# Constant matrix products, cued by results, in the recurrence of a two-layer decoder trunk

## The chip, the cores and the metric

The kernel runs on one core of a Trainium2 chip. Its time is the device time of one execution in microseconds (us). The kernel before was timed three times: 3217.7, 3225.27 and 3227.76 us, median 3225.27 us. The core has a matrix engine (PE; its weight loads are listed as PEld), a vector engine (DVE), an engine for activations and copies (ACT), a general one (POOL), and SP, whose queue issues nearly all DMA transfers. Each engine works through its instructions in order and waits at semaphores.

## The reference

Two layers over 1024 positions of width 1024. Each layer has a token mixer, a cross-attention into 256 memory rows and a SwiGLU network, each wrapped in RMS norms. Layer 0 mixes with a gated MLP, layer 1 with the recurrence that matters here:

```python
def rwkv7_recurrence(r, w, k, v, a, b):
    """S_t = S_{t-1} diag(w_t) + (S_{t-1} a_t) b_t^T + v_t k_t^T ;  y_t = S_t r_t."""
    def step(S, inp):
        r_t, w_t, k_t, v_t, a_t, b_t = inp
        sa = jnp.einsum('bhij,bhj->bhi', S, a_t)
        S = S * w_t[:, :, None, :] + sa[..., None] * b_t[:, :, None, :] + v_t[..., None] * k_t[:, :, None, :]
        return S, jnp.einsum('bhij,bhj->bhi', S, r_t)
    ...
y = rwkv7_recurrence(rh, decay, kh, vh, -kk, kk * ah)
mu = jnp.mean(y, axis=-1, keepdims=True)
var = jnp.mean(jnp.square(y - mu), axis=-1, keepdims=True)
y = (y - mu) * lax.rsqrt(var + RW_GN_EPS)
...
y = y + jnp.sum(rh * kh * r_k, axis=-1, keepdims=True) * vh
return (y * g) @ w_o
```

There are 16 heads of 64 values. The kernel computes the recurrence in chunks of 64 positions instead of step by step.

## The kernel before, in words

The large projections run as streams of 128x512 products, three for each pair of tiles (`mm3`, lines 148 to 150: high part by high part and the two mixed ones, in fp32r), and set most of the time. The recurrence works in four batches `b` of 256 positions, each with four groups `pi` of four heads. A batch goes through these steps, each written as a generator:

- `rwkv_prep`: loads the five inputs, forms the decay by a scan (L1295) and two exponentials (L1298, L1299), copies the decay of each chunk's end to `D` (L1302), builds the scaled tiles `ar` and `bk` (L1307 to L1311), and on PE a head sum (L1318), the chunk's inner products (L1330), transposes (L1337) and a product into `uv` (L1354). All PE products here are small and in fp32.
- `rwkv_solve`: inverts 32x32 triangles on DVE, 31 steps, two at a time for all heads, and stores the inverses.
- `rwkv_merge`: loads the inverses (`x<-scr` on L1393, `z<-scr` on L1398) and joins them to 64x64 with two rounds of 32x32 products (L1410, L1419), with copies between by ACT (L1413, L1422).
- `rwkv_chunks`: the sequential part over four chunks of eight states (L1433, L1446), with evacuations on ACT (L1453, L1462, L1465) and DVE (L1447).
- `rwkv_post`: the norm of the output. Sums (L1498, L1499), difference (L1502), squares (L1507), sums (L1511), a power on POOL (L208), products on POOL (L1503, L1513), transposes on PE (L1520, L1527), scaling on ACT and DVE (L1524, L1528, L1529), and a store (L1530).

After the chunks of batch `b - 1` and the solve of batch `b`, the loop runs the preparation of batch `b + 1` with the norm of batch `b - 1` in the background, and then the merge of batch `b`. So the span has three kinds of stretch: chunks; after the first and the second chunks a turn with norm, preparation and merge together; and, for the last batch, a merge between output projections.

Tiles in PSUM come from two rotating sets of four banks during the recurrence, `ps` (`bank`) and `ck` (`bank_ck`). A scheduler in the compiler places the instructions of each engine in an order that it estimates itself, so one more instruction can move its neighbours. SP's queue is in order too: a load that waits for a buffer holds those behind it.

## Time and profile before

| | us |
|---|---|
| median of three runs | 3225.27 |
| profiled execution, time | 3225.86 |
| profiled execution, span from first to last instruction | 3224.2 |
| PE busy in the span | 3085.9 |
| DVE busy | 1825.7 |
| ACT busy | 1485.6 |
| POOL busy | 824.9 |
| mean granted PE clock (1 is full) | 0.966 |

A row of a timeline has its start, its length, the engine, the source line, the operation, the tiles written and read, and the count of what was merged into the row; in brackets stands the engine's idle time before it and what ended it. In the rows by stretch each engine has its busy time and its count of instructions; the number after the five engines is the clock that PE was granted. A matrix product in fp32 is recorded as two.

### The profile page before, as it was taken

Reading aid. Unit: us, or ns where it says so; the run is one execution under the profiler, and the core shown is the slowest. Engines: PE = TensorE matmul, PEld = TensorE weight load, DVE = VectorE, ACT = ScalarE, POOL = GpSimd, SP = SyncE. Lnnn points to the kernel's source line nnn. Section 1 sums busy time; section 2 is a strip of 40 time slices with the busy share of each in tenths; the row PEclk is TensorE's granted clock in tenths of the full one; section 3 lists DMA queues with packets and bytes.
Section 4 is the critical chain, followed back from the end, with each engine's and each line's share of the span. In section 5 each row is a group of like instructions: output and inputs, shape, how many; then the busy total and the mean of one; then the engine's idle time right before and its main releaser. Section 6 shows DMA issues by size and latency. Waiting matters only on the chain.

```text
span 3224.2 us, 43854 instructions
## 1 busy us (share of the span) xinstructions
PE 3085.9 (96%) x16570; PEld 2523.5 (78%) x16570; DVE 1825.7 (57%) x2562; ACT 1485.6 (46%) x2751; POOL 824.9 (26%) x646
## 2 busy tenths in 40 slices
PE   8999999899999999999989999999999899999998
PEld 6888888778888777878767778787788678888776
DVE  5563544565555476655765665664545755554656
ACT  5442544543333345666653445455545533333443
POOL 0100011355555100111421121223011555554001
PEclk9999999999999999999998888899999999999999
DMA  5622634423333644744857642535544333333633
GB/s 188 207 77 67 201 122 161 144 66 104 105 98 99 243 142 131 222 122 151 260 190 194 192 107 81 153 96 179 175 153 142 100 102 98 98 98 114 237 112 134
DMA packets 432499, 456.54 MB, mean 142 GB/s; under 512 B 77664, under 2 KB 307200, under 8 KB 432288
## 3 DMA queue, kind: packets, MB, share of 16 engines
q1 hardware_dynamic: 425376, 428.57, 42.2%
q0 software_dynamic: 6912, 25.17, 2.4%
q8 instruction: 131, 2.15, 0.3%
q14 instruction: 80, 0.66, 0.1%
HBM read 331.43 MB, written 122.22 MB: 141 GB/s over the span
## 4 chain that ended last, share of the span: by engine, by line
PE 83%; DVE 7%; DMA 4%; ACT 2%; issue 2%; POOL 1%; SPq 1%; DVEq 0%; POOLq 0%; ACTq 0%
PE ps L438 25%; PE ps L148 12%; PE ps L149 12%; PE ps L150 12%; PE ps L639 11%; PE ck L1433 4%; DVE wl L119 2%; PE ps L1330 2%; PE ck L1446 1%; PE ps L1354 1%; DVE a L119 1%; ACT wh L118 1%; PE ps L262 1%; DMA a<-scr 1%; PE ps L1337 1%
## 5 line engine op out<-in xcount | busy, mean ns | idle before, releaser
L438 PE MATMUL ps<-a,wh 128*128 128x512 f32 x2464 | 772.6, 399 | 7.2 <-DVE a L119 5.0
L119 DVE TENSOR_TENSOR wl<-wr,wh 128x1024 fp32r<-128x1024 f32 (+1 forms) x417 | 478.9, 1158 | 485.9 <-ACT wh L118 477.7
L118 ACT CAST wh<-wr 128x1024 fp32r<-128x1024 f32 (+1 forms) x417 | 371.3, 902 | 621.7 <-PE ps L639 172.6
L438 PEld LDWEIGHTS ps<-a,wh 128*128 128x128 f32 x2464 | 465.6, 189 | 125.6 <-DVE a L119 7.3
L438 PE MATMUL ps<-a,wl 128*128 128x512 f32 x1232 | 480.3, 398 | 0.0
L148 PE MATMUL ps<-a,wh 128*128 128x512 f32 (+1 forms) x848 | 329.1, 393 | 11.3 <-ACT a L118 8.0
L149 PE MATMUL ps<-a,wh 128*128 128x512 f32 (+1 forms) x848 | 326.2, 386 | 2.4 <-DVE a L119 2.4
L148 PE MATMUL ps<-wh,a 128*128 128x512 f32 x800 | 316.4, 403 | 12.3 <-DVE a L1528 3.9
L150 PE MATMUL ps<-a,wl 128*128 128x512 f32 (+1 forms) x848 | 325.0, 385 | 0.8 <-DVE wl L119 0.8
L149 PE MATMUL ps<-wl,a 128*128 128x512 f32 x800 | 319.2, 399 | 0.8 <-DVE wl L119 0.8
L150 PE MATMUL ps<-wh,a 128*128 128x512 f32 x800 | 317.2, 400 | 0.0
L208 POOL TENSOR_TENSOR sm<-sm,mhalf 128x4 f32<-128x4 f32 (+3 forms) x60 | 70.0, 1170 | 922.0 <-DVE sm L228 846.4
L438 PEld LDWEIGHTS ps<-a,wl 128*128 128x128 f32 x1232 | 233.2, 189 | 57.3 <-DVE wl L119 0.9
L639 PE MATMUL ps<-wl,wh 128*128 128x512 f32 x588 | 233.0, 396 | 11.6 <-DVE wl L119 11.6
L119 DVE TENSOR_TENSOR wl<-s,wh 128x512 fp32r<-128x512 f32 x176 | 201.1, 1156 | 68.4 <-ACT wh L118 64.7
L639 PE MATMUL ps<-wh,wl 128*128 128x512 f32 x588 | 230.9, 393 | 0.0
L639 PE MATMUL ps<-wh 128*128 128x512 f32 x588 | 195.3, 395 | 15.1 <-ACT wh L118 15.1
L118 ACT CAST wh<-s 128x512 fp32r<-128x512 f32 x176 | 106.3, 620 | 201.8 <-PE ps L438 66.9
L148 PEld LDWEIGHTS ps<-a,wh 128*128 128x128 f32 x848 | 163.0, 193 | 44.0 <-ACT a L118 9.0
L148 PEld LDWEIGHTS ps<-wh,a 128*128 128x128 f32 x800 | 152.3, 191 | 49.5 <-DVE a L1528 4.3
L150 PEld LDWEIGHTS ps<-a,wl 128*128 128x128 f32 x848 | 163.0, 192 | 35.4 <-DVE wl L119 2.3
L149 PEld LDWEIGHTS ps<-a,wh 128*128 128x128 f32 x848 | 163.4, 193 | 32.9 <-DVE a L119 2.7
(280 smaller groups left out, 5338.2 us busy)
## 6 DMA issues: line engine op xcount, KB each, us to landing
scr<-a SPq DMA_DIRECT2D x218, 256.0 KB
wr<-in_ffn_w_in SPq DMA_DIRECT2D x90, 512.0 KB
wr<-scr SPq DMA_DIRECT2D x70, 512.0 KB
scr<-t SPq DMA_DIRECT2D x60, 512.0 KB
wr<-in_rw_w_rkv SPq DMA_DIRECT2D x48, 512.0 KB
a<-in_ffn_w_out SPq DMA_DIRECT2D x40, 512.0 KB
t<-scr SPq DMA_DIRECT2D x36, 512.0 KB
ld<-scr SPq DMA_DIRECT2D x72, 256.0 KB
```

What stands on the lines that cost most here:

```text
L118: self.nc.scalar.copy(hi, src)
L119: (engine or self.nc.vector).tensor_sub(lo, src, hi)
L148: nc.tensor.matmul(out, lhsT=ah, rhs=bh, start=start, stop=False)
L149: nc.tensor.matmul(out, lhsT=ah, rhs=bl, start=False, stop=False)
L150: nc.tensor.matmul(out, lhsT=al, rhs=bh, start=False, stop=stop)
L208: self.nc.gpsimd.tensor_tensor(out=r, in0=v, in1=self.mhalf[:, 0:n], op=ALU.pow)
L262: nc.tensor.transpose(ps[:, t * P:(t + 1) * P], xs[t][:, k * P:(k + 1) * P], self.ident)
L438: self.nc.tensor.matmul(out, lhsT=a, rhs=b, start=start and k == 0 and (i == 0), stop=k == 3 and i == 2, skip_group_check=True)
L639: nc.tensor.matmul(ps, lhsT=a, rhs=b, start=i in (1, 2, 5) and n == 0 and k == 0 and z == 0, stop=n == NS - 1 and k == steps[n][1] - 1 and ...
L1330: nc.tensor.matmul(ps[:, c * P:(c + 1) * P], lhsT=BK[hs, q * 4 + c, :, :], rhs=AR[hs, q * 4 + c, :, :], start=True, stop=True)
L1337: nc.tensor.transpose(ps[:, c * P:(c + 1) * P], BK[:, q * 4 + c, :, :], self.ident)
L1433: mm = lambda o, l, r: nc.tensor.matmul(o, lhsT=l, rhs=r, start=False, stop=True, skip_group_check=True)
```

## The change

A tile `fill` of 128x128 ones in bf16 is set at the start. A new function `dense(n, cue)` copies one column of `cue` into the first column of `fill` on ACT and then issues `n` products of `fill` with itself, read four times over (512 columns), into a fresh `ps` bank. Nothing reads that bank. The copy makes the products wait until `cue` is there; the value itself is used nowhere.

It is called in three places: in the preparation of batches 2 and 3 when `D` is there (six products), in every merge after the first of the four copies between its two rounds (six), and in the norm of batches 0 and 1 when the means are there (four). That is 8 × 6 + 4 × 6 + 8 × 4 = 104 products.

```diff
+        self.fill = self.const.tile([P, P], BF16, name='fill')
+        nc.gpsimd.memset(self.fill, 1.0)
...
+    def dense(self, n, cue):
+
+        nc = self.nc
+        nc.scalar.copy(self.fill[0:cue.shape[0], 0:1], cue)
+        ps = self.bank()
+        for _ in range(n):
+            nc.tensor.matmul(ps, lhsT=self.fill, rhs=self.fill.rearrange('p (o c) -> p o c', o=1).broadcast_to([P, 4, P]), start=True, stop=True)
...
@@ rwkv_prep
-        T = B['T'][pi] = {}
+        T, b_ = ({}, b)
+        B['T'][pi] = T
...
         nc.vector.tensor_copy(T['D'], ck(ee)[:, :, 63])
+        if b_ > 1:
+            self.dense(6, T['D'][:, 0:1])
...
@@ rwkv_merge
         for pi in range(4):
             nc.scalar.copy(tt[pi // 2][hi[pi], :], pb[pi][hi[pi], :])
             yield
+            if pi == 0:
+                self.dense(6, tt[0][hi[0], 0:1])
...
@@ rwkv_post
         nc.vector.tensor_scalar_mul(mu, mu, 1.0 / 64)
+        if b < 2:
+            self.dense(4, mu[:, 0:1])
```

The new lines shift the numbers: L1318 becomes L1331, L1330 L1343, L1337 L1350, L1354 L1367, L1393 L1406, L1398 L1411, L1410 L1423, L1520 L1537, L1527 L1544; the new products are on L113. Ahead of the recurrence the order of all engines is the same but for the memset. Three places show what moves.

PE at the end of the first chunks, where the turn begins. Before, from the first head sum of batch 2's preparation on (`sel` is its constant, `a` are norm tiles, `x` the inverses for the merge):

```order
L1318 MATMUL ps<-sel,ld 128x2 x4
L1330 MATMUL ps<-ar,bk 128x128 x8
L1520 MATMUL ps<-ident,a 128x128 x4
L1527 MATMUL ps<-ident,a 128x128 x4
L1337 MATMUL ps<-ident,bk 128x128 x4
L1520 MATMUL ps<-ident,a 128x128 x4
L1410 MATMUL ck<-x_15494 32x32 x12
```

Now, from the last product of the fourth norm's burst on:

```order
L113 MATMUL ps<-fill 128x512
L1343 MATMUL ps<-ar,bk 128x128 x4
L1537 MATMUL ps<-ident,a 128x128 x4
L1544 MATMUL ps<-ident,a 128x128 x4
L1350 MATMUL ps<-ident,bk 128x128 x4
L1537 MATMUL ps<-ident,a 128x128 x4
L1544 MATMUL ps<-ident,a 128x128 x4
L1343 MATMUL ps<-ar,bk 128x128 x4
L1537 MATMUL ps<-ident,a 128x128 x4
L1544 MATMUL ps<-ident,a 128x128 x4
L1343 MATMUL ps<-ar,bk 128x128 x4
L1423 MATMUL ck<-x_15560 32x32 x40
```

The merge's first products now stand behind two more groups of L1343 and behind the transposes of three norms instead of one and a half. Ahead of the head sum (now L1331) stand two norm bursts among the last chunk products and, directly before it, six and four products more, 18 in all; the fourth norm's four follow it after four products of L1343.

SP at the same turn, around the second load of the merge. Before (`invX` is the solve's result, `uv` a load for the preparation):

```order
L1384 DMA scr_9774<-invX 16x16x32 x4
L1495 DMA a<-scr_9792 128x2x128 x2
L1292 DMA ld<-scr_9787 128x2x256
L1393 DMA x_15494<-scr_9774 128x512
L1398 DMA z_14040<-scr_9773 32x16x32 x4
```

Now:

```order
L1397 DMA scr_9776<-invX 16x16x32 x4
L1510 DMA a<-scr_9794 128x2x128 x2
L1303 DMA ld<-scr_9789 128x2x256
L1361 DMA uv<-scr_9794 64x4x128 x2
L1303 DMA ld<-scr_9791 128x2x256
L1406 DMA x_15560<-scr_9776 128x512
```

The load of `x` has gone behind two loads of `uv` and one of `ld`. In the second turn its place is unchanged.

PE in the back of the second turn, between two groups of a preparation. Before:

```order
L1337 MATMUL ps<-ident,bk 128x128 x4
L1354 MATMUL ps<-uv,bk 64x64 x16
L1419 MATMUL ck<-z_14040,x1t 32x32 x3
L1318 MATMUL ps<-sel,ld 128x2 x4
L1419 MATMUL ck<-z_14041,x1t 32x32
```

Now:

```order
L113 MATMUL ps<-fill 128x512
L1434 MATMUL ck<-z_14042,x1t 32x32 x9
L1367 MATMUL ps<-uv,bk 64x64 x8
L1331 MATMUL ps<-sel,ld 128x2 x4
L1343 MATMUL ps<-ar,bk 128x128 x4
```

The next preparation's burst of six splits the sixteen products into `uv` in two groups of eight, and some of the merge's second round comes between. The bursts of the other preparations in a turn stand in the same way, and the merge's burst follows the last of them.

## The prediction

> **What bounds the kernel now.** I read the page first, for the share of each engine and the chain that ended last, then the busy time of the engines in stretches of the recurrence, then the PE's own timeline there.
>
> ```profile
> span 3224.2 us, 43854 instructions
> PE   8999999899999999999989999999999899999998
> PEclk9999999999999999999998888899999999999999
> PE 83%; DVE 7%; DMA 4%; ACT 2%; issue 2%; POOL 1%; SPq 1%; DVEq 0%; POOLq 0%; ACTq 0%
> ```
>
> The chain is 83% PE, and one fortieth of the span after the other has a PE that is busy for nine tenths. The second row of digits shows where it is not at full speed: slices 22 to 26 of 40, the recurrence. The stretches there (busy us and instructions of PE, PEld, DVE, ACT, POOL, then the granted clock, the DMA share and GB/s):
>
> ```profile
> core 0: us, PE busy (x) PEld busy (x) DVE busy (x) ACT busy (x) POOL busy (x), PEclk, DMA share, GB/s
> 1823.00:1843.60 20.60, 18.81 (x333) 17.42 (x334) 7.73 (x16) 7.00 (x14) 3.52 (x5) 0.50 0.80 199
> 1843.60:1900.40 56.80, 55.39 (x598) 46.08 (x596) 37.98 (x114) 33.86 (x110) 3.83 (x4) 1.00 0.24 65
> 1900.40:1914.70 14.30, 9.17 (x44) 7.22 (x40) 13.27 (x29) 5.70 (x12) 14.12 (x10) 0.54 0.66 158
> 1914.70:1928.90 14.20, 14.16 (x172) 11.30 (x173) 6.91 (x14) 3.72 (x7) 2.58 (x4) 0.50 0.77 192
> 1942.60:1967.90 25.30, 25.30 (x196) 22.42 (x194) 12.38 (x30) 7.37 (x14) 3.20 (x4) 0.53 0.39 112
> 2016.70:2031.00 14.30, 9.36 (x44) 7.42 (x43) 12.53 (x30) 5.50 (x12) 12.97 (x10) 0.53 0.62 160
> 2031.00:2045.00 14.00, 14.00 (x180) 11.58 (x181) 6.94 (x14) 4.90 (x9) 2.66 (x3) 0.50 0.79 211
> 2045.00:2075.30 30.30, 30.30 (x397) 27.07 (x396) 14.25 (x38) 10.81 (x22) 5.18 (x7) 1.00 0.68 180
> 2147.00:2164.50 17.50, 16.81 (x307) 15.59 (x306) 7.87 (x15) 9.22 (x22) 3.20 (x3) 0.71 0.45 137
> ```
>
> I call the stretch between two batches of chunks a turn: turn 1 from 1900.4 to 1967.9, turn 2 from 2016.7 to 2075.3. Each begins with a front of 14.3 us in which DVE (13.27, 12.53) and POOL (14.12, 12.97) work nearly without a gap and PE waits; after it PE never stops. Both halves run largely at half clock. The back of turn 2 is at 1.00, that of turn 1 mostly at half. Both turns do the same work (a preparation, a merge, a norm), so the pair prices the clock. PE at its beginning and end of the two (the number in brackets is the idle time before the row):
>
> ```profile
> 1914.74 0.54 PE L1410 MATMUL ck<-x 32*32 32x32 f32 x24 [2.51 <-DMA x<-scr]
> 1967.95 0.68 PE L1433 MATMUL ck<-rs,z 128*64 128x64 f32 x8
> 2030.99 0.55 PE L1410 MATMUL ck<-x 32*32 32x32 f32 x24 [2.35 <-DMA x<-scr]
> 2075.23 0.40 PE L1433 MATMUL ck<-rs,z 128*64 128x64 f32 x4
> 1931.33 1.16 PE L1330 MATMUL ps<-ar,bk 64*128 64x128 f32 x8
> 1945.97 2.07 PE L1330 MATMUL ps<-ar,bk 64*128 64x128 f32 x8
> ```
>
> From the merge's first product to the first of the next chunks it is 53.2 us in turn 1 and 44.2 us in turn 2: the half clock of one back costs 9.0 us. The same eight products take 1.16 us at full and 2.07 us at half.
>
> **What sets the clock.** Ahead of the recurrence PE runs 128x512 products alone, so their count in a clock window can be read:
>
> ```profile
> 1580.80:1584.20 3.40, 0.43 (x2) 0.00 (x0) 3.40 (x4) 0.57 (x1) 0.53 (x1) 1.00 0.85 236
> 1584.20:1587.60 3.40, 3.33 (x8) 2.67 (x9) 3.36 (x3) 0.02 (x2) 3.32 (x2) 0.50 0.88 202
> 1587.60:1591.00 3.40, 3.40 (x16) 2.74 (x15) 2.65 (x4) 3.40 (x6) 1.45 (x2) 1.00 0.81 202
> 1597.90:1601.30 3.40, 1.71 (x8) 1.09 (x7) 0.00 (x0) 1.50 (x2) 0.46 (x1) 1.00 1.11 375
> 1601.30:1604.70 3.40, 3.40 (x16) 2.71 (x16) 1.00 (x1) 2.66 (x4) 0.80 (x1) 1.00 1.01 344
> 1614.90:1618.30 3.40, 0.00 (x0) 0.00 (x0) 0.16 (x1) 3.37 (x6) 3.40 (x3) 1.00 0.98 340
> 1618.30:1621.70 3.40, 3.28 (x8) 2.61 (x9) 2.58 (x3) 1.81 (x4) 2.77 (x3) 0.50 0.98 327
> 1621.70:1625.10 3.40, 3.40 (x16) 2.76 (x15) 3.09 (x2) 2.50 (x4) 3.25 (x2) 0.99 0.97 302
> ```
>
> A window of 3.4 us with none or two of them is followed by one at 0.50; one with about eight, even at half clock, is followed by 1.00. But in 1942.60:1967.90 PE is busy for 25.30 of 25.30 us and stays at half. The groups of that stretch:
>
> ```profile
> L1330 PE MATMUL ps<-ar,bk 64*128 64x128 f32 x62 | 11.9, 408 | 0.0
> L1419 PE MATMUL ck<-z,x1t 32*32 32x32 f32 x70 | 3.2, 240 | 0.0
> ```
>
> Products of 64 or 32 rows and 128 or 32 columns seem to count for less than their time. So I read the clock as following how much of the array streams in a window, and six products of 128x512 come near what lifts it.
> [...]
>
> **The change, part by part.** It adds 104 products of 128x512 in 20 bursts: four of six (merges), eight of six (preparations of batches 2 and 3), eight of four (norms of batches 0 and 1). It removes nothing; it moves PE and SP work of the turns.
>
> *One product.* No row shows a bf16 product here. The nearest stream:
>
> ```profile
> 2740.40:2821.00 80.60, 80.60 (x346) 64.80 (x345) 42.02 (x46) 27.98 (x50) 40.97 (x28) 1.00 0.31 98
> ```
>
> 346 products in 80.60 us is 0.233 us each at full clock, 0.466 us at half. A burst of six is 1.4 or 2.8 us, one of four 0.93 or 1.9 us. A bf16 product could be shorter; it streams the same 512 columns, so I take 0.233 us and give the low end nothing for it.
>
> *Where the bursts stand.* By the new order each turn's front holds the four norm bursts and the first preparation's: 22 products, 5.1 us. Each turn's back holds three preparation bursts and the merge's (in turn 1 as chunks begin again): 24 products, 5.6 us. The merges of batches 0 and 3 hold six each: 2×22 + 2×24 + 12 = 104.
>
> *Fronts.* PE waits there today, by these rows and the 2.51 and 2.35 us above:
>
> ```profile
> 1903.83 2.07 PE L1330 MATMUL ps<-ar,bk 64*128 64x128 f32 x8 [0.48 <-DVE sm L1511]
> 1910.07 1.11 PE L1337 MATMUL ps<-ident,bk 128*128 128x128 f32 x4 [2.19 <-DVE sm L1511]
> 2020.24 2.07 PE L1330 MATMUL ps<-ar,bk 64*128 64x128 f32 x8 [0.44 <-DVE sm L1511]
> 2026.26 1.11 PE L1337 MATMUL ps<-ident,bk 128*128 128x128 f32 x4 [1.96 <-DVE sm L1511]
> ```
>
> That is 5.2 us in turn 1 and 4.8 us in turn 2, set by DVE and a load, so the 22 products of a front cost nothing that ends last; if that cover is gone they cost 2 × 5.1 = 10.3 us. The gain lies right behind: 14.2 us (1914.70 on) and 14.0 us (2031.00 on) of PE work without a gap at 0.50. At full clock each would be 7 us shorter. I take 6.5 us each, half a microsecond less for the window in which the burst first has to count. The new order in turn 1 also lets PE do two more groups of norm transposes and two of L1330 before it waits for the merge's load. Ends: 0 (DVE at 13.27 of 14.30 us sets the pace and the clock falls again between bursts) to 7.1 and 7.0.
>
> *Backs.* Turn 1 comes to what turn 2 already has: −9.0 us. The bursts then cost 5.6 us in each back, since PE has no gap there: 30.30 of 30.30 us. Ends of a back's 24 products: 5.6 to 11.2 us.
>
> *Merges 0 and 3.* Merge 0 lies in 20.6 us at 0.50. Its burst stands behind L1330's first products, at about 1830.5, so windows from 1833.4 on can be full: 10.2 us of work come to 5.1, less 2.8 us for six products at half clock, −2.3 us net. In merge 3 the clock of 0.71 over 17.5 us means 10.2 us at half; the burst comes in the middle of it and I give it half of the 5.1 us that a full clock would bring, 2.6, less 1.4 us: −1.2 us.
>
> *Cues.* Twenty casts of one column on ACT, like this one:
>
> ```profile
> 1902.66 0.16 ACT L1320 COPY bo<-ps 128x8 f32<-128x8 f32 x1
> ```
>
> 20 × 0.16 = 3.2 us, on an engine with 5.70 us of work in a front of 14.30 and 33.86 in 56.80 of chunks: hidden; with no cover, 3.2 us. Each cast also waits for its cue and for the previous burst's reads of the same tile, and behind it on ACT stand the evacuations that PE waits for in the chunks. The cues (sums, a decay column) are ready before the casts come up in ACT's order, so I take 0; the other end is one burst, 0.9 us, for each of the eight norm casts, 7.5 us. The memset of the constant at the start lies on POOL, idle there, and costs nothing; uncovered, less than 1 us.
>
> *The bank.* A burst takes one of four rotating `ps` banks and nobody reads it, so the next user waits only for PE, which is in order anyway. Its own first product can wait for DVE's L1511 as PE does above.
>
> **Sum**, against the profiled execution (span 3224.2, time 3225.86 us, 0.6 from the median of 3225.27, so taken as one): −2.3 (merge 0) −6.5 −9.0 +5.6 (turn 1) −6.5 +5.6 (turn 2) −1.2 (merge 3) = −14.3. That gives 3211.6, say **3212 us**.
>
> **Rivals.**
>
> A, *the fronts give nothing.* DVE and POOL set their pace and PE's 14 us behind go back to half between bursts, which lie up to ten microseconds apart there. The 13 us of the fronts drop out: 3225.9 − 14.3 + 13 = 3224.6. For it: the two fronts' DVE rows. Against: from 1914.70 DVE is busy for 6.91 of 14.20 us only, so PE sets the pace there.
>
> B, *the loads come late: slower.* The place is SP's queue in a front. SP waits for PE's L1318, which frees a load buffer, and the merge's load is queued behind:
>
> ```profile
> SPq L1292 <- PE ps L1318: 8.6, 2, 5.9
> SPq L1393 <- DVE invZ L1377: 2.9, 1, 2.9
> 1914.31 1.24 SPq L1348 DMA_DIRECT2D uv<-scr  x2
> 1915.65 0.55 SPq L1292 DMA_DIRECT2D ld<-scr  x1
> ```
>
> Eighteen products now stand ahead of that L1318: 18 × 0.233 = 4.2 us in each turn. In turn 1 the merge's second load also moves behind three others, 1.24 + 0.55 = 1.8 us. If all of it reaches PE, 2 × 4.2 + 1.8 = 10.2 us, and PE that waits longer loses the fronts' 13 us as well: 3211.6 + 23.2 = 3234.8; if half of those eighteen run at half clock, 2 × 2.1 = 4.2 us more: 3239. It decides from a lateness of 2.9 us on, the wait for DVE that the merge's first load has anyway and that hides less than that. For it: 4.2 is above 2.9. Against: the bursts begin before PE's last chunk products, which wait themselves.
>
> C, *constant products don't lift the clock*, so the change doesn't do what it says: all cost, 11.2 + 5.6 in the backs and 2.8 + 2.8 in the merges, 3248. Against: the row at 1618.30, where eight products of this size lifted it. They were of other types and data.
> [...]
>
> D, *more than the sum.* PE's waits go too, since faster transposes free DVE and the loads earlier: 10 us more, 3202.
>
> **How the numbers follow.** Forecast 0.47, A 0.28, B 0.15, C 0.06, D 0.04. A measurement of this kernel tells about 0.3% from no change, 9.7 us: faster is below 3215.6, slower above 3234.9. My forecast lies 3.6 us inside, so 0.07 of it I put to the same; A lends 0.06 to faster, B 0.03 to the same. Faster: 0.40 + 0.06 + 0.04 = 0.50. Same: 0.07 + 0.22 + 0.03 = 0.32. Slower: 0.12 + 0.06 = 0.18. The forecast's own range is 3200 to 3222 (the fronts' and merges' ends); with A and most of B, 3198 to 3233 leaves out C, a part of B and the far end of D, under 2 in 10.
>
> **What would show it.** Right: the clock of the backs near 1.00 in both turns, the 53.2 us of turn 1 near 43 with bursts, L1330 at 1.16 us for eight behind both fronts, the chunks as long as now. A: the 14 us behind the fronts still at 0.50. B: PE waiting over 4 us for `x<-scr`. C: bursts of six taking 2.8 us with no 1.00 behind them. The forecast is wrong if the turns together are not at least 8 us shorter, or if the time lies outside the turns and merges.

## The result, and the profile after

The changed kernel takes 3239.41 us (median of five executions, 3234.8 to 3242.54) where the kernel before takes 3225.27 us. The ratio is 1.0055, with a 95% interval of 1.0035 to 1.0075: slower by half a per cent, and outside the forecast range of 3198 to 3233 us. The profiled execution has a span of 3240.8 us and a time of 3242.54 us.

The page of the changed kernel, the lines that answer to those shown of before (span, granted clock in 40 slices):

```profile
span 3240.8 us, 44085 instructions
PEclk9999999999999999999999899899999999999999
```

The dent in the clock is smaller: two slices at 8 where before had five. So the constant products did what they were put there for, and the time went up all the same.

To see where, the recurrence is cut at five products that both kernels have: the first product of merge 0, and the last state product (`ck<-s,ar`) of each of the four batches of chunks. That makes four stages: merge 0 with the chunks of batch 0, turn 1 with those of batch 1, turn 2 with those of batch 2, and merge 3 with those of batch 3. Busy time by stretch of the kernel before (us, then busy us and instructions of PE, PEld, DVE, ACT and POOL, then the granted clock, the DMA share and GB/s):

```profile
1823.80:1895.00 71.20, 69.56 (x876) 59.80 (x876) 40.43 (x115) 37.20 (x112) 4.61 (x6) 0.86 0.38 96
1895.00:2011.30 116.30, 110.00 (x1122) 92.67 (x1121) 71.96 (x187) 53.81 (x150) 27.71 (x23) 0.78 0.41 110
2011.30:2123.10 111.80, 104.92 (x1146) 88.01 (x1146) 74.57 (x197) 54.08 (x151) 24.78 (x22) 0.88 0.48 131
2123.10:2201.60 78.50, 77.81 (x850) 65.90 (x849) 33.37 (x71) 45.59 (x128) 19.75 (x14) 0.93 0.35 95
```

The same four stretches of the changed kernel:

```profile
1824.30:1903.00 78.70, 76.10 (x881) 64.68 (x882) 41.59 (x115) 37.77 (x113) 4.66 (x6) 0.81 0.32 87
1903.00:2019.20 116.20, 112.40 (x1180) 89.01 (x1180) 76.32 (x196) 57.61 (x163) 27.04 (x23) 0.94 0.41 113
2019.20:2135.90 116.70, 111.49 (x1167) 89.15 (x1167) 69.94 (x183) 54.37 (x155) 23.88 (x21) 0.90 0.45 121
2135.90:2217.60 81.70, 81.48 (x871) 66.56 (x871) 34.56 (x76) 46.00 (x131) 18.50 (x15) 0.96 0.32 95
```

| stage | before, us | after, us | difference | forecast |
|---|---|---|---|---|
| merge 0, chunks 0 | 71.2 | 78.7 | +7.5 | −2.3 |
| turn 1, chunks 1 | 116.3 | 116.2 | −0.1 | −6.5 −9.0 +5.6 = −9.9 |
| turn 2, chunks 2 | 111.8 | 116.7 | +4.9 | −6.5 +5.6 = −0.9 |
| merge 3, chunks 3 | 78.5 | 81.7 | +3.2 | −1.2 |
| all that lies ahead of and behind them | 2846.4 | 2847.5 | +1.1 | 0 |

The differences add up to +16.6 us, those forecast to −14.3. Further profiles of both kernels (experiment 6) place the loss: the four stages together took 371.5 to 381.0 us in five executions of the kernel before, and 393.3 and 397.7 us in two of the changed kernel; the rest took 2833.5 to 2846.4 us before and 2847.5 and 2840.2 us after, so it moves by more than ten microseconds with nothing changed. The stage with the largest gain in clock, turn 1 (0.78 to 0.94), gained nothing; the first stage lost both clock and time.

*Merge 0.* PE's timeline in the changed kernel (start, us, instruction, idle time before it and what ended it):

```profile
1831.29 2.64 PE L113 MATMUL ps<-fill 128*128 128x512 bf16 x6
1836.64 2.08 PE L1434 MATMUL ck<-z,x1t 32*32 32x32 f32 x118
1841.55 3.80 PE L1367 MATMUL ps<-uv,bk 128*64 128x64 f32 x32 [2.24 <-ACT bt L1351]
```

The windows there:

```profile
1833.70:1837.10 3.40, 3.40 (x53) 2.89 (x53) 0.58 (x2) 0.00 (x0) 0.00 (x0) 1.00 1.08 335
1837.10:1840.50 3.40, 2.21 (x106) 1.93 (x98) 1.46 (x2) 0.15 (x1) 1.59 (x3) 1.00 0.27 56
1840.50:1843.90 3.40, 2.35 (x21) 2.36 (x22) 3.37 (x7) 2.25 (x5) 1.71 (x2) 0.50 0.08 27
1843.90:1861.00 17.10, 17.10 (x96) 15.51 (x95) 6.45 (x16) 5.77 (x12) 0.00 (x0) 0.50 0.42 111
```

The burst lifts the clock for two windows. PE runs through the merge's small products (118 of them in 2.08 us), meets a wait, and the clock falls again. For another 17.1 us it then stays at 0.50 with PE busy all the time, where the kernel before ran at 1.00 over the same microseconds:

```profile
1843.60:1861.00 17.40, 17.12 (x181) 14.77 (x181) 8.43 (x26) 9.19 (x26) 0.00 (x0) 1.00 0.43 108
```

What PE waited for lies three steps back. DVE and ACT in the changed kernel:

```profile
1839.04 1.22 DVE L1306 TENSOR_TENSOR_SCAN ld<-chunk_on,ld 128x512 f32<-128x512 bf16 x1 [4.76 <-DMA ld<-scr]
1840.35 0.63 ACT L1309 ACTIVATE tt<-ld 128x512 f32<-128x512 f32 x1 [7.39 <-DVE ld L1306]
1840.88 0.57 ACT L1351 COPY bt<-ps 128x512 f32<-128x512 f32 x1
```

DVE stands at the next preparation's scan until its load has landed, ACT stands behind that scan, and the evacuation `bt` that frees PE comes after it in ACT's order. In the kernel before ACT waits at the same place for as long (7.53 us, until 1840.64), but this evacuation stands ahead of the wait:

```profile
1832.52 0.59 ACT L1338 COPY bt<-ps 128x512 f32<-128x512 f32 x1
```

So the wait came with the new order: the burst stands ahead of the transposes that `bt` copies (they start at 1833.76, before at 1830.50), and the copy has moved behind the load. Nor is the wait needed for the loss. In after_four_all (experiment 1), which has the same burst, PE waits for no more than 0.86 and 0.34 us here; the clock falls after one window, and the stage takes 79.6 us. What the cases share is that the clock falls over the small products behind the burst; experiment 3 counts them.

*Turns.* The end of the chunks of batch 0 and the front of turn 1 in the changed kernel, and two rows of turn 2's front:

```profile
1909.17 1.47 PE L113 MATMUL ps<-fill 128*128 128x512 bf16 x6
1910.97 1.04 PE L113 MATMUL ps<-fill 128*128 128x512 bf16 x4 [0.33 <-ACT fill L110]
1912.73 1.16 PE L1343 MATMUL ps<-ar,bk 64*128 64x128 f32 x8
1920.00 1.11 PE L1350 MATMUL ps<-ident,bk 128*128 128x128 f32 x4 [3.04 <-DVE sm L1528]
1922.75 2.07 PE L1343 MATMUL ps<-ar,bk 64*128 64x128 f32 x8
...
2038.02 0.50 PE L1423 MATMUL ck<-x 32*32 32x32 f32 x36 [3.84 <-DMA x<-scr]
2041.68 2.07 PE L1343 MATMUL ps<-ar,bk 64*128 64x128 f32 x8
```

The first eight products of L1343 take 1.16 us, full clock, in the front itself. Behind the wait for DVE (3.04 us), or in turn 2 for the load (3.84 us), eight of them take 2.07 us: the clock is low once more, for 13.7 us in turn 1 and 10.2 us in turn 2. In the last 3.4 us ahead of the fall PE is busy for 1.33 us in turn 1 (1915.63 to 1919.04) and for 0.48 us in turn 2 (2035.09 to 2038.50), and for 2.21 us at the wait of 2.24 us in merge 0 (1837.10 to 1840.50), where small products fill the rest.

### The profile page after: what moved, and what is told of

It is laid out like the page before. It is cut to its first block, busy times and chain, and to the rows that moved or that the text cites. A ratio compares the mean times of both kernels' runs of the same rounds, so it can differ in the third digit from the quotient of the medians.

```text
span 3240.8 us, 44085 instructions
## 1 busy us (share of the span) xinstructions
PE 3104.6 (96%) x16674; PEld 2525.8 (78%) x16674; DVE 1826.6 (56%) x2562; ACT 1490.5 (46%) x2771; POOL 820.5 (25%) x647
## 4 chain that ended last, share of the span: by engine, by line
PE 82%; DVE 7%; DMA 4%; ACT 3%; issue 2%; POOL 1%; SPq 1%; DVEq 0%; POOLq 0%; ACTq 0%
PE ps L448 25%; PE ps L158 11%; PE ps L159 11%; PE ps L160 11%; PE ps L649 11%; PE ck L1448 4%; DVE wl L129 2%; PE ps L1343 2%; PE ck L1461 1%; PE ps L1367 1%; DVE a L129 1%; PE ps L272 1%; PE ps L113 1%; DMA scr<-a 1%; ACT wh L128 1%
```

## The experiments

Ratios are against the kernel before on the same chip, with 95% intervals. The recurrence is the sum of the four stages, 377.8 us in the first profile of the kernel before.

**1. The order of the chunks, alone and taken away.** The code of the chunks is not touched by the change, yet the products of batch 1 stand in another order. PE in the kernel before, a piece of these chunks:

```profile
1986.55 0.71 PE L1446 MATMUL ck<-s,ar 128*128 128x128 f32 x4
1987.19 0.45 PE L1433 MATMUL ck<-rs,z 128*64 128x64 f32 x4
1987.57 0.49 PE L1446 MATMUL ck<-s,ar 128*128 128x128 f32 x2
1987.98 0.45 PE L1433 MATMUL ck<-rs,z 128*64 128x64 f32 x4
```

And in the changed kernel:

```profile
1985.14 0.49 PE L1461 MATMUL ck<-s,ar 128*128 128x128 f32 x2
1985.56 0.45 PE L1448 MATMUL ck<-rs,z 128*64 128x64 f32 x4
1985.94 0.49 PE L1448 MATMUL ck<-s,ident 128*128 128x128 f32 x2
...
1986.85 0.49 PE L1461 MATMUL ck<-s,ar 128*128 128x128 f32 x2
```

Before, the products of up to four states are gathered by kind; after, one state follows another, with a change of shape at each step and 1.71 us from one `s,ar` to the next. From the fifth to the 29th state (the ninth record of `s,ar`, since each of these products leaves two, to the 57th) it is 1974.3 to 2007.1 before, 1.37 us per state, and 1973.2 to 2014.1 after, 1.70 us. Two kernels force an order by edges between successive chunk products (of the class `NoSync`): before_state gives the kernel before the new order in batch 1, after_four_all gives the changed kernel the old order in batches 1 to 3. That old order is one of groups of four in batches 1 and 3; in batch 2 it goes mostly by pairs (1.48 us per state), and there it is the changed kernel that has groups of four (1.36 us). So where an expectation says groups of four for batch 2, read the order of the kernel before; and its "ninth state" is the ninth record, the fifth state.

```diff
+        if b in _ORDER:
...
+            for x, y in zip(keys, keys[1:]):
+                self.tc.add_manual_dep(rec[y].ins, rec[x].ins.name, mybir.DependencyInfo(mybir.DependencyClass.NoSync, mybir.DependencyReason.DATA), reason='order')
```

> The kernel before, without any burst, its only edit being that the chunk products of batch 1 are issued in the order that they have in the changed kernel: state by state, where before has groups of four states. Theory 'order': the interleaving of shapes alone makes these chunks about 9 us longer (some 1.36 to 1.7 us per state), so 3232 to 3236 us, with all before the second half of the chunks of batch 1 as in the kernel before. Rival 'bursts': the chunks of batch 1 are slower in the changed kernel because of what the bursts do (clock, engines, buffers), so the order alone gives 3225 us, within 3.

> The changed kernel with all its 104 products, but the chunk products of batches 1 to 3 are issued in the order of the kernel before (groups of four). Theory 'order': 8 to 10 us come back in the chunks of batch 1, 3229 to 3232 us. Rival 'bursts': 3239 us, within 3.

Measured: before_state 3254.27 us, ratio 1.0097 (1.0067 to 1.0126); after_four_all 3222.83 us, 1.0008 (0.9992 to 1.0025). The four stages of before_state:

```profile
1827.20:1898.80 71.60, 69.16 (x875) 59.35 (x876) 40.36 (x115) 37.16 (x111) 4.48 (x6) 0.86 0.37 96
1898.80:2024.00 125.20, 118.71 (x1130) 97.35 (x1131) 73.35 (x190) 55.69 (x152) 28.53 (x23) 0.78 0.39 104
2024.00:2143.30 119.30, 110.34 (x1137) 92.25 (x1137) 73.69 (x194) 53.53 (x149) 25.39 (x21) 0.84 0.43 120
2143.30:2234.30 91.00, 90.09 (x850) 74.80 (x849) 32.86 (x71) 45.32 (x128) 19.23 (x15) 0.79 0.30 83
```

And of after_four_all:

```profile
1819.00:1898.60 79.60, 78.00 (x882) 65.90 (x882) 40.58 (x115) 37.60 (x113) 4.76 (x6) 0.79 0.32 87
1898.60:2007.90 109.30, 105.01 (x1168) 85.25 (x1167) 73.51 (x191) 54.79 (x159) 25.89 (x23) 0.94 0.43 117
2007.90:2120.80 112.90, 109.67 (x1192) 88.07 (x1192) 72.03 (x186) 55.50 (x160) 26.98 (x22) 0.95 0.47 129
2120.80:2201.60 80.80, 78.80 (x856) 65.27 (x855) 34.61 (x79) 45.59 (x129) 18.28 (x14) 0.94 0.32 94
```

The rival falls on both sides. The order alone costs 8.9 us in turn 1 with its chunks (125.2 against 116.3, at the same clock of 0.78), and taking it out of the changed kernel brings 6.9 us there (109.3 against 116.2, both at 0.94). From the fifth state to the last `s,ar`, where both run at full clock, it is 45.0 against 37.0 us and 45.9 against 37.3. Both kernels moved by more than expected. In before_state the order of batch 3 became another one too, and the clock fell in turn 2 and in the chunks of batch 3 (0.84 and 0.79 for these stages where before has 0.88 and 0.93), 20 us more. In after_four_all the old order was also given back to batches 2 and 3, 3.8 and 0.9 us. In batch 2 this is no gain per state: there the first state product comes 48.5 us after the chunks of batch 1 where the changed kernel has 66.5, and products of the turn, 32 into `uv` and a burst, run among the chunks. Why it comes so much earlier is open. Which property of the state-by-state order costs the 0.33 us per state (a reload of weights, a change of the tile's shape) was not tried.

**2. Without the burst of merge 0.**

```diff
+        mi = self.mi = getattr(self, 'mi', -1) + 1
...
-            if pi == 0:
+            if pi == 0 and mi in (1, 2, 3):
```

> The changed kernel without the burst in the merge of batch 0; 98 products are left. Theory 'relapse': that burst lifts the clock for one or two windows, PE gets ahead of DVE and ACT, waits, and the windows that follow are too empty to keep the clock, so that the chunks of batch 0 begin 8.7 us later than before; without it they begin as before, 8 to 11 us earlier than in the changed kernel: 3228 to 3231 us. Rival 'bursts': it costs its own PE time only, six products at 0.23 to 0.47 us: 3236 to 3238 us.

Measured: 3230.12 us, ratio 1.0030 (1.0012 to 1.0049), where the changed kernel has 1.0055: 8 us less. The stage takes 71.3 us, as before, where the changed kernel took 78.7 and after_four_all 79.6: a burst of 1.4 to 2.8 us cost 7.4. That the burst costs more than its own products holds beyond this pair: in the three profiles with it the stage took 78.7, 79.5 and 79.6 us, and in twelve without it nine times 70.5 to 71.6, twice 75.4 and once 77.8 us. So it is not the only cause of a late merge 0 (see 4). The theory's way there, PE that gets ahead and waits, is not shown by this pair: without the burst the copy `bt` is also back in its old place, and after_four_all loses the clock with hardly a wait.

**3. The same PE time without the lift.** Each constant product reads one row of the array instead of 128. one_row_state keeps the changed kernel's chunk order, one_row_four has the order of before.

```diff
-            nc.tensor.matmul(ps, lhsT=self.fill, rhs=self.fill.rearrange('p (o c) -> p o c', o=1).broadcast_to([P, 4, P]), start=True, stop=True)
+            nc.tensor.matmul(ps, lhsT=self.fill[0:1, :], rhs=self.fill[0:1, :].rearrange('p (o c) -> p o c', o=1).broadcast_to([1, 4, P]), start=True, stop=True)
```

> The changed kernel, its chunk products pinned to its own order, with each of the 104 products reading one row of the constant where the change reads 128: the same 512 columns and the same bank. Theory 'rows': the clock follows how many rows and columns of the array stream, so one-row products lift nothing: the front of turn 1 is as before (27.4 us from the last select to the first state product of the preparation, where the changed kernel has 21.0), its back takes the 40.1 us of before plus 24 products at 0.23 to 0.47 us, 46 to 51 us where the changed kernel has 30.2; merge 0 has no relapse, 6 to 8 us back. Together 3253 to 3263 us. Rival 'busy': any product that keeps PE busy counts in full, 3239 us within 4.

> The changed kernel with one-row products, as in one_row_state, and the chunks of batches 1 to 3 in groups of four. It has the PE time of the change without its lift and without its order. Theory: 104 products cost PE 24 us at full clock and up to 48 at half and are hidden in no wait: 3245 to 3262 us; the other 40 us and more of one_row_state were state-by-state chunks that could not leave half clock. Rival 'the fronts hide theirs', as forecast (44 of the 104 free): 14 to 28 us, 3236 to 3249.

Measured: one_row_state 3303.32 us, ratio 1.0257 (1.022 to 1.0294); one_row_four 3292.0 us, 1.0215 (1.016 to 1.027). Both are above every number that had been expected. The groups of constant products, first of the changed kernel, then of one_row_four:

```profile
L113 PE MATMUL ps<-fill 128*128 128x512 bf16 x104 | 29.6, 423 | 0.7 <-ACT fill L110 0.7
```

```profile
L119 PE MATMUL ps<-fill 1*128 1x512 bf16 x104 | 40.2, 538 | 0.5 <-ACT fill L116 0.5
```

The four stages of one_row_four, and its longest stretch at half clock in turn 1:

```profile
1826.00:1899.50 73.50, 73.14 (x882) 61.52 (x882) 40.46 (x115) 37.82 (x114) 4.67 (x6) 0.85 0.35 93
1899.50:2048.80 149.30, 140.79 (x1171) 109.94 (x1171) 75.11 (x202) 56.42 (x161) 23.52 (x21) 0.69 0.32 89
2048.80:2204.70 155.90, 151.04 (x1187) 119.16 (x1187) 68.44 (x175) 55.44 (x157) 26.56 (x23) 0.66 0.33 91
2204.70:2288.40 83.70, 81.72 (x857) 67.92 (x855) 34.72 (x79) 45.65 (x129) 18.59 (x14) 0.90 0.32 90
...
1930.60:1995.50 64.90, 59.28 (x374) 47.92 (x375) 22.59 (x51) 15.78 (x32) 4.67 (x5) 0.50 0.39 108
```

PE is busy for 59.28 of 64.90 us and stays at 0.50. The one-row products fill PE's time there and the clock stays low; that they also leave less room for the other products in the same 3.4 us fits the sums that follow. The rival 'busy' is dead, and so is the estimate that the damage would end at the products' own time. The clock records of before and of the change hold 1.00 and 0.50 alone, so from the clock of the quoted rows the time at half clock is 2 × (1 − clock) × length: over the four stages 109 us before and 237 us in one_row_four. Half of the difference is 64 us, 104 × 0.233 are 24.2 us, together 88; the recurrence grew from 377.8 to 462.4, by 84.6. So nearly all of the products' time is paid, and almost nothing of it lies in waits.

The traces show clock and products side by side. In all 18 profiles the steps of the clock around the recurrence lie on a grid of 3.413 us. For each window of this grid between the first product of merge 0 and the last state product of batch 3, add up over the recorded products the columns streamed times the share of the 128 rows in use (a product that crosses an edge is divided by its time). Of 2073 windows, 98.4% are divided by one line drawn through these sums: at 1565 or more the next window is at 1.00, below it at 0.50. In the first profiles of before and of the change it is 226 of 227; the one left has a sum of some 1585 (from 1898.23 us in before) and is followed by 0.50. The line was fitted to the same windows, so it is a description of them. Columns without rows get 88.8% right at best, weighted also with the array's columns in use 93.2%, and PE's busy share 77.4%, while 72.4% of the windows are followed by 1.00 in any case. In merge 0 of the changed kernel the window with the burst has 3085 and the next ones 1973 and 1274, where the clock falls; in after_four_all they have 3126 and 1397.

The same sum of clock and products for the others: half of the change in half-clock time, plus 0.233 us for each constant product, beside what the recurrence did.

| kernel | half clock, us | half of the change | products | sum | recurrence, us | left over |
|---|---|---|---|---|---|---|
| before | 109 | | 0 | | 377.8 | |
| after | 74 | −17.6 | +24.2 | +6.6 | 393.3 (+15.5) | +8.9 |
| after_four_all | 68 | −20.7 | +24.2 | +3.5 | 382.6 (+4.8) | +1.3 |
| before_state | 152 | +21.3 | 0 | +21.3 | 407.1 (+29.3) | +8.0 |
| skip0_four | 48 | −30.7 | +22.8 | −7.9 | 374.7 (−3.1) | +4.8 |
| one_row_four | 237 | +64.2 | +24.2 | +88.4 | 462.4 (+84.6) | −3.8 |

In these rows 8 to 9 us are left over where the chunks of batch 1 go state by state, and within 5 us of nothing where they go in groups of four. Of the other profiles skip0 and after_again (state by state) leave 7 to 8 us, t1_all_four, t1_lite13_four and skip0_four_again (groups) 1 to 3. Two do not fit: t1_back_four leaves some 13 us in groups of four, 6 of them in waits that PE has in addition, and one_row_state −8 us state by state. So the sum is no law. For the change it fits what experiment 1 shows directly: it buys 17.6 us of clock, pays 24.2 us of products for it, and pays 8 to 9 us for an order.

**4. Repairs.** skip0_four has no burst in merge 0 and the chunks in the order of before, as the three others have. t1_all_four has bursts in turn 1 only (46 products); t1_back_four leaves out its norm bursts as well; t1_lite13_four has t1_all_four's with two of the four preparation bursts (34 products). The conditions of preparation, merge and norm in t1_all_four, against the changed kernel:

```diff
-        if b_ > 1:
+        if b_ == 2:
...
-            if pi == 0:
+            if pi == 0 and mi in (1,):
...
-        if b < 2:
+        if b == 0:
```

t1_lite13_four has `b_ == 2 and pi % 2` in the first of them; t1_back_four has the first two and no norm burst.

> The changed kernel with both repairs: no burst in merge 0, and the chunk products of batches 1 to 3 in groups of four. Theory 'three terms' (order, relapse and bursts add up): skip0 was 9.3 us below the changed kernel, after_four_all some 16, together 25 below 3239: 3211 to 3217 us. Rival 'luck of the windows' (each repair only shifts the phase of the clock's windows, so the second adds nothing): 3221 to 3226 us.

> Bursts in turn 1 alone (norm of batch 0, preparation of batch 2, merge of batch 1), chunk products in groups of four. Theory: merge 0 and turn 2 as in the kernel before, turn 1 as in after_four_all, where it took 8 us less from the end of the chunks of batch 0 to the ninth state of batch 1: 3212 to 3217 us. Rival 'turn 2 needs its bursts too': no less than skip0_four plus 5 us, 3217 to 3222.

> As t1_all_four, without the norm bursts. Theory 'products at the tail are on the path': the 16 norm products cost 4 to 6 us ahead of the merge's first product and bring 6.4 us behind it, so leaving them out changes the time by less than 3 us against t1_all_four. Rival 'hidden', as forecast: they cost nothing, and without them the front of turn 1 is 6.5 us longer: t1_all_four plus 5 to 7 us.

> As t1_all_four, with preparation bursts for two of the four head pairs: 34 products, all in turn 1, every chunk in the order of before. Theory 'gain and price cancel' (t1_all_four has 46 products, 10.7 us of PE, for a gain of about that): 12 products fewer, 2.8 us, and the back holds its clock once lifted, as turn 2 of the kernel before does without any burst: 3216 to 3221 us, against 3222 before. Rival 'each burst is needed': the back falls to half in between and it is 3223 to 3228 us.

Measured: skip0_four 3224.58 us, ratio 1.0000 (0.9983 to 1.0017); t1_all_four 3223.89 us, 1.0005 (0.9987 to 1.0024); t1_back_four 3232.18 us, 1.0028 (1.0012 to 1.0044); t1_lite13_four 3237.55 us, 1.0060 (1.0037 to 1.0083). None is faster than the kernel before. The stages of skip0_four's profiled execution, which at 3214.17 us was the fastest of its twelve:

```profile
1820.40:1891.30 70.90, 69.72 (x876) 59.93 (x876) 40.42 (x115) 37.23 (x112) 4.56 (x6) 0.86 0.37 97
1891.30:2001.30 110.00, 103.03 (x1167) 82.59 (x1167) 73.26 (x191) 54.71 (x158) 26.06 (x22) 0.97 0.43 116
2001.30:2113.90 112.60, 109.35 (x1191) 87.99 (x1192) 73.95 (x186) 55.61 (x160) 26.35 (x22) 0.95 0.48 130
2113.90:2195.10 81.20, 79.30 (x857) 65.45 (x855) 34.74 (x79) 45.65 (x129) 18.88 (x14) 0.94 0.32 93
```

Even here turn 1 gains 6.3 us, turn 2 costs 0.8 us and merge 3 costs 2.7 us. The theory that the three repairs add up gave 3211 to 3217 and failed at the median; its rival's 3221 to 3226 was met. t1_back_four lost 8.3 us against t1_all_four, which speaks for the rival (5 to 7 us) and against the theory that gain and price of the norm bursts cancel. It is less than proof, since the intervals of the two ratios overlap; the stage itself shows it in one profile of each, 117.1 us at a clock of 0.90 against 108.9 at 0.95, with 9.2 and 4.4 us in which PE is idle. t1_all_four, whose profiled execution was with 3214.49 us near the lowest of its twelve, met neither of its ranges at the median. t1_lite13_four, above the numbers of both theories, shows how little margin there is: with twelve products fewer the back of turn 1 was at half clock for 23.9 us again and the stage took 122.6 us, 6.3 more than before, where t1_all_four took 108.9.

> A second profiled execution of skip0_four, whose first was 8 us below its median. Theory 'position against the clock windows': with not one instruction changed, single stretches of the recurrence (a front, a back, the merge of batch 0) differ by 3 to 10 us between the two executions, each with its own list of half-clock windows, and the chunks at full clock agree within 0.5 us. Rival 'noise everywhere': the difference is spread evenly over the kernel.

The second execution of skip0_four took 3225.23 us. Its stages are 77.8, 110.3, 109.0 and 83.8 us: merge 0 late by 6.9 us without a burst there, turn 1 the same within 0.3, turn 2 shorter by 3.6, merge 3 longer by 2.6. Chunks that ran at full clock in both agree within 0.5 us. So for the four stages what the theory of position against the clock windows foretold came, and merge 0 was late at a lower clock without a burst (0.77 for the stage, 0.86 in the first execution). Of the 11 us between the two executions 6 lie there; the other 5 lie ahead of and behind the stages, which the theory says nothing of.

**5. Cues without products.** Each product streams 2 columns, where the change streams 512.

```diff
-            nc.tensor.matmul(ps, lhsT=self.fill, rhs=self.fill.rearrange('p (o c) -> p o c', o=1).broadcast_to([P, 4, P]), start=True, stop=True)
+            nc.tensor.matmul(ps[:, 0:2], lhsT=self.fill, rhs=self.fill[:, 0:2], start=True, stop=True)
```

> All bursts and cues of the change, but each product streams 2 columns where the change streams 512, so that the casts, the waits and the bank stay and the PE time and the lift go; its chunk products of batch 1 are in groups of four as in before, those of batches 2 and 3 as in the changed kernel. Theory: cues cost nothing, 3222 us within 4, and up to 11 us more if the order of batch 3 lets the clock fall there as it did in before_state. Rival 'cues and waits cost' (each of 20 casts holds PE or ACT): some 10 us more at the fronts of the turns, where the norm casts are, 3230 to 3240.

Measured: 3227.55 us, ratio 1.0038 (1.0008 to 1.0068), twelve executions from 3219 to 3258 us. The profiled one has 73.3, 119.3, 111.2 and 80.9 us, 7 us above the kernel before, 3.0 of it in turn 1. The casts of the cues and the waits for them in the changed kernel:

```profile
L110 ACT CAST fill<-sm 128x1 bf16<-128x1 f32 x8 | 1.5, 188 | 2.3 <-ACT s L1480 1.6 <-PE ps L113 0.7
L110 ACT CAST fill<-D 128x1 bf16<-128x1 f32 x8 | 1.5, 192 | 7.4 <-PE ps L113 7.4
```

ACT waits 7.4 us in all ahead of the preparation's casts until PE has read the constant of the burst before. That is the wait that the forecast named. What it costs at the end lies between 0 and 7 us and isn't settled: the small products take some PE time of their own, the chunks of batch 3 are in another order (36.3 us from the fifth state to the last where before has 34.6), and the spread of this kernel is wide.

**6. Further executions of the kernel before and of the change.** Nothing is edited.

> A second profiled execution of the kernel before, with the same question as in skip0_four_again. Theory: the turns and the merges of batches 0 and 3 differ by 3 to 10 us each, in both directions, and the chunks agree within 0.5 us; the back of turn 1, which was at half clock for 23.9 us in the first profile, need not be so here. Rival: the half clock of that back belongs to the program and is here again, 23 to 25 us of it.

> A third profiled execution of the kernel before. Theory: the back of turn 1 is at half clock in some executions and at full in others, with nothing changed, which moves the chunks of batch 1 by 9 us. Rival: the second execution, where it was at full, was the exception; here it is at half for 23 to 25 us.

> A fourth profiled execution of the kernel before, with the expectation of before_3.

> A fifth profiled execution of the kernel before, with the expectation of before_3.

> A second profiled execution of the changed kernel. Theory: the chunks of batch 1 again take about 9 us more between their ninth and last state than in the kernel before (46 us where before has 37), since that is the order; the chunks of batch 0 again begin late after a relapse in merge 0, since the window behind its burst is again too empty; the turns may differ by 3 to 10 us. Rival 'luck': one or both of these are gone here.

Measured: 3216.37, 3222.12, 3221.07 and 3212.85 us for the kernel before, 3239.57 us for the change. In before_again the back of turn 1 was at full clock with no burst:

```profile
1942.60:1967.90 25.30, 24.23 (x307) 21.14 (x307) 14.14 (x38) 12.91 (x31) 3.20 (x4) 1.00 0.51 142
```

Its turn 1 with chunks took 106.9 us where the first profile has 116.3, and turn 2 took 115.2 where that has 111.8; merges 0 and 3 moved by less than half a microsecond, against the theory. The sums of experiment 3 differ at the back's first fall: 1454 in the first profile, with PE busy throughout and the next window at 0.50, and 1614 here, with the next at 1.00. In before_3, before_4 and before_5 turn 1 with its chunks took 115.6, 116.0 and 115.9 us, with 23.9 us at half clock in the same place. So four of five executions have the slow back and the rival of those three texts was met: the term was a property of the kernel, most of the time. after_again repeats both findings: 79.5 us in merge 0 with chunks (78.7; turn 2 and merge 3 took 116.5 and 85.8), and 45.9 us from the fifth state of batch 1 to its last `s,ar`, the same as in the first profile, where before has 37.0.

## Why the prediction was wrong, by its own steps

In the prediction's own terms, the gains by the clock were to be 29.7 us (5.1 in merge 0, 15.5 in turn 1, 6.5 in turn 2, 2.6 in merge 3). By the half-clock time of each stage about 17 came: a loss of 5.0 in merge 0, then gains of 18.8, 1.7 and 1.7. The products were to cost 15.4 us, since those of the fronts were put at nothing, and cost 24.2. The order of the chunks had no term and cost 8 to 9 us.

*What sets the clock: right for these profiles.* Behind bursts of six that began at 0.50 the clock was 1.00 (in the changed kernel those at 1831.29 in merge 0, 2065.77 in turn 2 and 2171.35 us in merge 3; in turn 1 all began at 1.00). Rows and streamed columns agree with the next window's clock in 98.4% of the windows, PE's busy share in 77.4%. Rival C is refuted by the clock of the stage of turn 1, 0.78 before and 0.94 after; with one-row products it was 0.69. The price of a product was right as well: a burst of six takes 1.40 us of PE at full clock (1934.20 to 1935.60 in the changed kernel), 0.233 us each. What was missing is how little six products hold: in merge 0 the two windows behind the burst's own have sums of 1973 and 1274, in turn 2's back the window behind a burst has 1113, and the clock falls after the 1274 and after the 1113.

*Turn 1's gain: right in kind, too large.* The stage gained 6.0 to 7.4 us in the four profiles where its chunks kept their order and the same bursts (109.3, 110.0, 110.3, 108.9 against 116.3); the forecast was 9.9. In the changed kernel the fifth state came 9.1 us earlier (70.2 us behind the chunks of batch 0, before 79.3): half-clock time fell from 51.2 to 13.7 us, worth 18.8 us, less 10.7 us for 46 products. The order then took it away. One execution of the kernel before had the gain without any burst (106.9 us).

*"The chunks as long as now": the step that failed most plainly.* It stood among the signs and had no term in the sum. It was worth 8.9 us in the stage of turn 1 (before_state), 6.9 in the changed kernel. The forecast looked at the new order only in the turns, where the bursts stand.

*Merge 0: the sign was wrong.* −2.3 us was forecast, +7.5 came, and without that burst the stage is 71.3 us. The step took the windows behind the burst as full until the work ended. It did not ask whether the clock stays at 1.00 over the small products behind the burst (118 in 2.08 us), nor what the burst moves: the transposes and their copy `bt`, which came to stand behind a load that lands when it lands. Half-clock time of the stage went from 20 to 30 us.

*Fronts: "cost nothing that ends last" failed.* PE's waits in a front were to cover 22 products, 5.1 us. Turn 1's waits went from 5.2 us to 3.4 (0.33 and 3.04), turn 2's from 4.8 to 4.2 (0.33 and 3.84): 1.8 and 0.6 us were covered. Over the four stages PE's idle time went from 15.5 to 11.8 us, so 3.7 of the 24.2 us of products took the place of a wait. Two norm bursts of each turn stand among the last chunk products, where PE has no gap, and the waits behind are set by DVE (in turn 1 it ended 15.1 us behind the last `s,ar` before the change and 17.0 after) and by the load (in turn 2, 19.7 and 18.8 us). So the priced other end, 2 × 5.1 us, was nearer. How much of it is really paid is open, since without the norm bursts PE idles for 9.2 us in turn 1's stage where it otherwise idles for 4.4 (t1_back_four, t1_all_four). The gain of 6.5 us by the clock did come: the first stretch at half clock of each turn, 27.3 us before, lasted 13.7 us in turn 1 and 10.2 us in turn 2, worth 6.8 and 8.5 us. But it came in the fronts more than behind them, where DVE and the load set the end: L1330's eight products were to take 1.16 us behind both fronts and took 2.07 behind both waits.

*Turn 2's back: +5.6 forecast.* With −6.5 for the front it made −0.9; the stage came out at +4.9, and up to the fifth state of the chunks it was +9.5 (77.8 against 68.3). The back, at 1.00 before, was at half for 13.7 us in the change, with PE never waiting there: the window behind the turn's second preparation burst had a sum of 1113 (2052.15 to 2055.56). So the half-clock time of the turn went from 27.3 to 23.9 us only, worth 1.7 us, against 9.8 us for the 42 products that lie in the stage. With the old order of the chunks, some of which then run among the turn's products, the stage took 112.9 us.

*Merge 3: −1.2 forecast, +3.2 measured.* Its burst stands four microseconds ahead of the chunks, takes 2.74 us at half clock, and has hardly anything to speed up. Of the 3.2 us, 2.3 lie behind the fifth state (36.9 us to the last, before 34.6), where the order of these chunks changed as well.

*Cues: 0 forecast, 0 to 7 us, open.*

*Rivals.* B, late loads, gave 3234.8 to 3239 us and so nearly the right time by luck, for the wrong reason: its sign, a wait over 4 us for `x<-scr`, was absent in turn 1 and 3.84 us in turn 2. A's sign, half clock behind the fronts, came in part (13.7 and 10.2 us of 27.3): between the last burst of a front and the first of the back the clock fell, at a wait. The signs that were named against the forecast came true: the turns together, up to the fifth state of the next chunks, took 79.3 + 68.3 us before and 70.2 + 77.8 after, no shorter, and 7.5 us more lie in merge 0's stage.

## What to carry to other kernels

Work that is added only to keep the clock up should be priced in full unless a named wait shrinks by that much; here 24 us of products bought 18 us of clock, and no selection of the bursts that was tried made a faster kernel. Where a scheduler sets the order, look at the order of the costly loops that the change does not touch as well, since a stage's gain of 7 us was undone there by a reordering of untouched code. And behind each place that gets faster ask which load or which engine is met next: here the clock was at half again for 13.7 and 10.2 us behind the waits in the two fronts, and for 20.5 us in merge 0 behind the burst's small products.

## What the runs showed of the hardware that had not been expected

- In these 18 profiles the clock went with how much of the array streams more than with how long PE is busy. Columns times the share of rows, summed over a window of 3.413 us, agree with the next window's clock in 98.4% of 2073 windows (line at 1565, fitted to them), PE's busy share in 77.4%. With 104 one-row products PE was busy for 59.28 of 64.90 us at 0.50, and the kernel took 1.0215 times as long.
- The same 24 states of fp32 products took 1.37 us each in groups of four and 1.70 us one after another, at full clock and with hardly a gap on PE (0.4 and 0.0 us in all).
- Half clock lasted where the work was of small products: of the windows at half clock that were followed by another, half have sums under 1098, while half of those at full clock that kept it have over 2936. The kernel before stayed at half for 23.9 us in turn 1's back in four of five executions and not at all in the fifth, with no instruction changed.
- The spread of this program is wide: 35 executions of the kernel before on one chip lie between 3209 and 3241 us. That back explains only a part, since the time outside the four stages moved by 13 us between five profiles; what moves there is open.
